# The scores of a retention's first 128 keys from float32r halves instead of float32

## The chip, the cores and the metric

The kernel runs on one core of one Trainium2 chip. The metric is the time of one execution on the device in microseconds; the number given for a kernel is the median of its runs. A profile is one execution recorded by the hardware profiler; its span runs from the first to the last instruction. Names of engines: PE is TensorE's matmul stream, PEld its weight loads, DVE is VectorE, ACT is ScalarE, POOL is GpSimd, SP is SyncE, which here only issues transfers.

## What is computed

The reference is one inference step of a two-layer streaming encoder for a prompt of 256 frames and 32 further frames of a running stream. Layer 0 mixes tokens by gated spatial mixing, layer 1 by retention with 8 heads; behind each comes a SwiGLU network, and every residual sum is normalised. All data are float32. The retention, cut to what matters here:

```python
q = rope(heads(q, RET_DK), pos) * (RET_DK ** -0.5)       # RET_DK = 256
k = rope(heads(k, RET_DK), pos)
v = heads(v, RET_DV)                                     # RET_DV = 512
...
scores = jnp.einsum('bhqd,bhkd->bhqk', q, k) * decay[None]
intra = jnp.einsum('bhqk,bhkv->bhqv', scores, v)
cross = jnp.einsum('bhqd,bhdv->bhqv', q, s0) * inner[None, :, :, None]
s_new = blk_decay[None, :, None, None] * s0 + jnp.einsum('bhkd,bhkv->bhdv', k * zeta[None, :, :, None], v)
```

The kernel takes the prompt's 256 frames as one block with masked decay, so the scores of a head are: the first 128 keys with all 256 queries, the second 128 keys with the last 128 queries, and 32 sample keys with 32 sample queries.

## The kernel before

**Float32 through halves.** A float32 product of two operands runs on TensorE at a fraction of the speed of its reduced form float32r. Nearly all products of the kernel are therefore made of three float32r products: an operand is split into a high half (a cast to float32r, on ACT, L437) and a low half (the float32 value less the high half, on DVE, L438), and high x high, low x high and high x low are summed in PSUM (`step`, L106 to L108). The function `split` makes both halves. A few small products are left in plain float32; each shows in the profile as two records.

**The stream of weights.** All weights lie in one packed array in the order in which they are used, 8 blocks of 128 x 128 to a chunk. `prep` fetches a chunk on SP's queue into `raw`, and `split` makes `whi` and `wlo`; it is called three chunks ahead. A chunk feeds 24 matmuls. ACT's cast of a chunk waits until TensorE has let go of an older chunk's tile. Every chunk costs ACT one cast and DVE one subtraction of 1024 columns.

**The order.** TensorE's instructions are in the order in which the program writes them. On ACT and DVE a scheduler orders them when the program is built; each engine works through its list in order. A matmul names the results that it waits for, and what stands behind it on TensorE waits with it.

**The retention.** Its projection `b_in` makes, for each head, two row blocks of k, two of q (128 rows by 288 columns each: 256 prompt and 32 sample frames), four of v and four of the gate. When a block of 16 products of three is done, `evac` is called and then a tick is counted; `core.after(n, f)` calls f after n ticks, so a tick is the time of one block. When both blocks of k or of q are there, `turn` rotates them on DVE (`rope`, L655 to L660: rt1 and rt2, the first 128 rows of the result, rt1 and rt2 again, the second rows) into a float32 tile `rk` or `rq`. For k it transposes the rows (`tk`), which POOL's queue writes to DRAM (`k_room`) and reads back turned (`kw`); from these `k_split` makes `kh`, `kl` and `ks`, with casts on ACT (L741, L747) and subtractions on DVE (L743, L749). For q it makes `qf` and its two halves `qi`, and asks for `scores` two ticks later (three in head 0, whose `turn` is itself two ticks late).

**The scores.** `scores` (L757 to L761) makes the three score blocks with six float32 products, two for each block, one for each 128 rows of q and k. DVE multiplies them with the decay (`pf`, L766 to L768), ACT and DVE split the result, and `attend` and `attend_prompt` multiply it with v, with products of 512 columns (L623 is the helper `wide`, which views the columns in fours).

**The small tiles.** `PostNorm.tmp` gives a tile of 128 x 320 float32 from a ring of six (tag `tmp` in the pool `lnp`). The normalisations use it for sums and squares; the start of `b_in` uses it for the corrected blocks `fix`. From the turn of head 0 to the normalisation's end behind `b_out` nothing else used it.

## Time and profile before

| what | value |
|---|---|
| median of 3 runs | 2780.95 us (2780.55 to 2782.05) |
| span of the profiled execution | 2779.0 us |
| instructions | 51384 |
| PE, DVE, ACT, POOL busy | 100%, 61%, 45%, 5% |
| HBM, over the span | 184 GB/s |
| matmul of 288 columns, recorded length | 288 to 289 ns |
| scores of all heads, first and last start | 1211.5 to 1810.2 us |

The profiled execution has no other time than its span; the median of the runs is 1.95 us above it, for what lies before the first and behind the last instruction. Matmul records overlap: the next one starts before the recorded length is over. What a matmul takes from TensorE is therefore read from start to start. In a row of the timeline stand the start, the length, the engine, the line, the operation with what it writes and reads, and how many were merged; idle time of the engine before it stands in brackets with what ended it.

### The profile page before, as it was taken

What the parts mean: (1) busy time and instruction counts of PE and PEld (TensorE: products, weight loads), DVE (VectorE), ACT (ScalarE), POOL (GpSimd) and SP (SyncE); (2) the same over time, 40 slices, a digit from 0 to 9 for tenths busy, and PEclk for the clock granted to TensorE, in tenths of its full rate; (3) what the DMA queues carried; (4) which work ended last, traced back from release to release, by engine and by line L of the source; (5) the groups of instructions that cost most, each with busy time, mean ns of one, the idle gap of its engine ahead of it and who ended that gap; (6) DMA issues with size and microseconds to landing.
All of it is one profiled execution on the core that took longest, in us unless ns stands there. A gap on an engine that the chain in (4) does not pass through costs nothing.

```text
span 2779.0 us, 51384 instructions
## 1 busy us (share of the span) xinstructions
PE 2767.0 (100%) x21574; PEld 2754.2 (99%) x21574; DVE 1691.7 (61%) x2414; ACT 1236.9 (45%) x1635; POOL 141.4 (5%) x241
## 2 busy tenths in 40 slices
PE   9999999999999999999999999999999999999998
PEld 9999999999999999999999999999999999999998
DVE  6688964445444466867765666767854445444465
ACT  5455553333343344644543444445643433333343
POOL 1100000000000000022200111200000000000001
PEclk9999999999999999999999999999999999999999
DMA  8655555555555555577765666765555555555553
GB/s 285 213 186 166 169 172 174 172 173 175 175 174 173 175 177 176 168 224 232 234 194 175 195 220 215 229 194 172 169 173 175 175 174 172 172 174 174 175 175 125
DMA packets 146584, 515.49 MB, mean 185 GB/s; under 512 B 18016, under 2 KB 20336, under 8 KB 146320
## 3 DMA queue, kind: packets, MB, share of 16 engines
q1 hardware_dynamic: 131984, 473.47, 52.3%
q0 software_dynamic: 14224, 38.59, 4.5%
q8 instruction: 168, 2.75, 0.4%
q14 instruction: 64, 0.52, 0.1%
q10 hardware_dynamic: 144, 0.15, 0.0%
HBM read 486.98 MB, written 25.17 MB: 184 GB/s over the span
## 4 chain that ended last, share of the span: by engine, by line
PE 99%; DVE 0%; issue 0%; ACT 0%; DVEq 0%; POOL 0%; POOLq 0%
PE af_in L107 13%; PE af_in L108 13%; PE af_in L106 13%; PE ab_in L107 7%; PE ab_in L106 7%; PE ab_in L108 7%; PE af_out L108 6%; PE af_out L106 6%; PE af_out L107 6%; PE aa_in L108 2%; PE ab_out L108 2%; PE ab_out L106 2%; PE aa_in L107 2%; PE aa_in L106 2%; PE ab_out L107 2%; PE aa_out L107 1%
## 5 line engine op out<-in xcount | busy, mean ns | idle before, releaser
L438 DVE TENSOR_TENSOR wlo<-raw,whi 128x1024 fp32r<-128x1024 f32 (+1 forms) x892 | 1086.1, 1219 | 871.5 <-ACT whi L437 866.5
L437 ACT CAST whi<-raw 128x1024 fp32r<-128x1024 f32 (+1 forms) x892 | 931.6, 1046 | 1376.6 <-PE af_in L107 326.6
L107 PE MATMUL af_in<-xl,whi 128*128 128x288 f32 (+1 forms) x2816 | 813.9, 289 | 0.0
L108 PE MATMUL af_in<-xh,wlo 128*128 128x288 f32 (+1 forms) x2816 | 813.7, 289 | 0.0
L106 PE MATMUL af_in<-xh,whi 128*128 128x288 f32 (+1 forms) x2816 | 813.0, 289 | 0.0
L108 PEld LDWEIGHTS af_in<-xh,wlo 128*128 128x128 f32 x2816 | 527.7, 187 | 0.0
L107 PEld LDWEIGHTS af_in<-xl,whi 128*128 128x128 f32 x2816 | 527.7, 187 | 0.0
L106 PEld LDWEIGHTS af_in<-xh,whi 128*128 128x128 f32 x2816 | 527.7, 187 | 0.0
L107 PE MATMUL ab_in<-xl,whi 128*128 128x288 f32 (+1 forms) x1536 | 444.3, 289 | 0.0
L106 PE MATMUL ab_in<-xh,whi 128*128 128x288 f32 (+1 forms) x1536 | 444.2, 289 | 0.0
L108 PE MATMUL ab_in<-xh,wlo 128*128 128x288 f32 (+1 forms) x1536 | 443.6, 289 | 0.0
L106 PE MATMUL af_out<-hh,whi 128*128 128x288 f32 x1408 | 405.9, 288 | 0.0
L107 PE MATMUL af_out<-hl,whi 128*128 128x288 f32 x1408 | 405.9, 288 | 0.0
L108 PE MATMUL af_out<-hh,wlo 128*128 128x288 f32 x1408 | 405.9, 288 | 0.0
L107 PEld LDWEIGHTS ab_in<-xl,whi 128*128 128x128 f32 x1536 | 287.9, 187 | 1.1
L106 PEld LDWEIGHTS ab_in<-xh,whi 128*128 128x128 f32 x1536 | 287.9, 187 | 0.9
L108 PEld LDWEIGHTS ab_in<-xh,wlo 128*128 128x128 f32 x1536 | 287.8, 187 | 0.0
L106 PEld LDWEIGHTS af_out<-hh,whi 128*128 128x128 f32 x1408 | 263.8, 187 | 0.0
L107 PEld LDWEIGHTS af_out<-hl,whi 128*128 128x128 f32 x1408 | 263.8, 187 | 0.0
L108 PEld LDWEIGHTS af_out<-hh,wlo 128*128 128x128 f32 x1408 | 263.8, 187 | 0.0
L106 PE MATMUL aa_in<-xh,whi 128*128 128x288 f32 x512 | 148.3, 290 | 0.0
L108 PE MATMUL aa_in<-xh,wlo 128*128 128x288 f32 x512 | 147.7, 288 | 0.0
(242 smaller groups left out, 2896.1 us busy)
## 6 DMA issues: line engine op xcount, KB each, us to landing
raw<-in_wpack_dram SPq DMA_DIRECT2D x887, 512.0 KB, 3.4
v_room<-tv POOLq DMA_DIRECT2D x32, 144.0 KB, 4.9
of<-o_room POOLq DMA_DIRECT2D x32, 144.0 KB, 4.8
vw<-v_room POOLq DMA_DIRECT2D x8, 512.0 KB, 5.9
out_st_s_dram<-sso POOLq DMA_DIRECT2D x16, 256.0 KB, 2.8
o_room<-to POOLq DMA_DIRECT2D x8, 512.0 KB, 3.6
out_st_p_dram<-so POOLq DMA_DIRECT2D x16, 256.0 KB, 5.2
y<-in_xT_dram SPq DMA_DIRECT2D x8, 288.0 KB, 5.1
```

The costliest lines, as they stand in the source:

```text
L106: mm(ps, hi, xh, start=first, stop=False)
L107: mm(ps, hi, xl, start=False, stop=False)
L108: mm(ps, lo, xh, start=False, stop=last)
L437: nc.scalar.copy(hi, f)
L438: nc.vector.tensor_tensor(lo, f, hi.bitcast(F32), ALU.subtract)
```

## The change

Every head's k and q, as far as the first score block needs them, are split into halves right behind the rotation: k's first 128 columns of both row blocks in one split, q's 256 prompt columns in a split for each row block. The six halves (two of k, four of q) lie in the ring of small tiles of the normalisations. The first score block is then made of six float32r products in the view in fours: for each of the two row blocks high x high, q's low with k's high, and q's high with k's low. The other two score blocks stay in float32.

```diff
+    def room(self, name, dt=F32R):
+        return self.lnp.tile([P, ROW], dt, tag="tmp", name=name, bufs=6)
+
     def tmp(self, name, dt=F32):
-        return self.lnp.tile([P, ROW], dt, tag="tmp", name=f"{name}_{self.gi}", bufs=6)[:, LEAD:LEAD + NT]
+        return self.room(f"{name}_{self.gi}", dt)[:, LEAD:LEAD + NT]
...
                 if isk:
                     self.kr = r
+                    self.kt = [ln.room(f"kt{i}_{h}")[:, 40:40 + 2 * P].rearrange("p (d n) -> p d n", d=2) for i in range(2)]
+                    split(nc, *self.kt, r[:, :, :P])
...
                     self.qr = r
+                    self.qt = [[ln.room(f"qt{i}{d}_{h}")[:, LEAD:LEAD + NP] for i in range(2)] for d in range(2)]
+                    for d in range(2):
+                        split(nc, *self.qt[d], r[:, d, :NP])
...
                 for d in range(2):
-                    mm(b[:, 0:NP], self.kr[:, d, 0:P], self.qr[:, d, 0:NP], start=d == 0, stop=d == 1)
+                    for i, (j, q) in enumerate(((0, 0), (0, 1), (1, 0))):
+                        wide(b[:, 0:NP], self.kt[j][:, d, :], self.qt[d][q], start=d == 0 and i == 0, stop=d == 1 and i == 2)
```

In the built program the instructions of TensorE, POOL and SP keep their order but for the two float32 products that become six; ACT's list has three casts more a head and DVE's three subtractions more, and in head 2 one pair of neighbours on DVE is exchanged.

## The prediction, made before the result was known

> **What bounds the kernel now.** The page of the kernel before was read first, then who waits for whom on TensorE, then the stretches around the scores of each head, engine by engine.

> ```profile
> span 2779.0 us, 51384 instructions
> PE 2767.0 (100%) x21574; PEld 2754.2 (99%) x21574; DVE 1691.7 (61%) x2414; ACT 1236.9 (45%) x1635; POOL 141.4 (5%) x241
> ...
> PEclk9999999999999999999999999999999999999999
> ...
> PE 99%; DVE 0%; issue 0%; ACT 0%; DVEq 0%; POOL 0%; POOLq 0%
> ```

> TensorE is busy all the time at full clock, and the chain that ended last is TensorE for 99%. Its waits are one, at the start:

> ```profile
> PE warm L937 <- POOL g_nrm L486: 1.0, 1, 1.0
> ```

> So TensorE is the clock of this kernel: what it is spared is gained whole, and whatever it must wait is lost whole, since nothing later has slack to give it back. VectorE at 61% looks free, but this is a mean. Seven microseconds around the start of the scores look like this (the heads with numbers 1, 2 and 7; columns: PE, PEld, DVE, ACT, POOL busy, clock, DMA share, GB/s):

> ```profile
> 1270.00:1277.00 7.00, 7.00 (x56) 6.90 (x55) 6.60 (x15) 4.05 (x7) 0.00 (x0) 1.00 0.67 218
> 1327.00:1334.00 7.00, 7.00 (x56) 6.90 (x55) 6.60 (x17) 3.96 (x7) 0.00 (x0) 1.00 0.62 205
> ...
> 1805.00:1812.00 7.00, 7.00 (x56) 6.89 (x55) 6.35 (x17) 4.58 (x9) 0.00 (x0) 1.00 0.47 162
> ```

> There VectorE is over 90% busy, right where the change gives it work on which TensorE will wait.

> **The products, removed and added.** Scores of head 2 on TensorE (start, length, operation; the x4 are two fp32 products of two records each):

> ```profile
> 1330.73 0.29 PE L108 MATMUL ab_in<-xh,wlo 128*128 128x288 f32 x1
> 1330.86 1.02 PE L757 MATMUL sc<-rq,rk 128*128 128x256 f32 x4
> 1331.72 0.61 PE L759 MATMUL sc<-rq,rk 128*128 128x128 f32 x4
> ```

> What is removed holds TensorE from 1330.86 to 1331.72: 0.86 us a head. In its place stand six float32r products of 256 columns. The trace has that form once, in the sample's mixing, two products from 139.58 to 139.82, so 0.12 us each; beside it float32r of 288 columns and of 512:

> ```profile
> 139.58 0.41 PE L546 MATMUL smix<-g_v,g_w 96*128 96x256 f32 x2
> 139.82 0.30 PE L106 MATMUL aa_in<-xh,whi 128*128 128x288 f32 x1
> 139.96 0.29 PE L107 MATMUL aa_in<-xl,whi 128*128 128x288 f32 x1
> 140.09 0.29 PE L108 MATMUL aa_in<-xh,wlo 128*128 128x288 f32 x1
> ...
> 1395.97 0.39 PE L623 MATMUL os<-whi,qi 128*64 128x512 f32 x1
> 1396.19 0.39 PE L623 MATMUL os<-wlo,qi 128*64 128x512 f32 x1
> ```

> Start to start, 288 columns take 0.13 us and 512 take 0.22, half of which is 0.11. I take 0.12, bounds 0.11 and 0.13: six take 0.72 us (0.66 to 0.78). Alone that is a gain of 0.14 us a head, 1.1 us over eight. L759 and L761 stay as they are, with their one change back to float32r.

> **The splits, and who waits.** Each head adds three casts on ScalarE and three subtractions on VectorE, 256 columns each.

> ```profile
> L437 ACT CAST xh<-y 128x288 fp32r<-128x288 f32 x64 | 26.6, 430 | 17.0 <-PE af_in L108 8.1 <-DMA y<-in_xT_dram 5.4 <-PE ab_in L108 3.4
> L766 DVE TENSOR_TENSOR pf<-sc,dec 128x256 f32<-128x256 f32 x8 | 3.3, 417 | 0.0
> ```

> That is 0.42 us for a subtraction (L766 has its size) and about 0.40 for a cast (430 ns for 288 columns): 10 us in all on each engine, free as long as nobody waits. k's halves are made before q is there at all, and q's first halves with rq; nobody waits for these. q's second low half is the case. As built, VectorE's order in heads 1 to 7 is: rt2q, low half of q's first 128 rows, rq, qf, wlo, four kl, two ks, low half of q's second rows, qi. TensorE needs that last half for its fifth product. VectorE and ScalarE before, head 2:

> ```profile
> 1327.49 0.45 DVE L659 TENSOR_TENSOR rt2q<-ab_in,r_cs 128x288 f32<-128x288 f32 x1
> 1327.97 0.46 DVE L660 TENSOR_TENSOR rq<-rt1q,rt2q 128x288 f32<-128x288 f32 x1
> 1328.46 0.22 DVE L712 TENSOR_TENSOR qf<-rq,r_inn 128x64 f32<-128x64 f32 x1
> 1328.97 1.23 DVE L438 TENSOR_TENSOR wlo<-raw,whi 128x1024 fp32r<-128x1024 f32 x1 [0.28 <-ACT whi L437]
> 1330.11 1.14 DVE L743 SCALAR_TENSOR_TENSOR kl<-kw,r_zt,kh 128x128 fp32r<-128x128 f32 x4
> 1331.26 0.61 DVE L749 SCALAR_TENSOR_TENSOR ks<-kw,r_zt,ks 32x128 fp32r<-32x128 f32 x2
> 1331.90 0.23 DVE L438 TENSOR_TENSOR qi<-qf,qi 128x64 fp32r<-128x64 f32 x1
> ```

> ```profile
> 1327.88 1.05 ACT L437 CAST whi<-raw 128x1024 fp32r<-128x1024 f32 x1 [1.94 <-PE ab_in L107]
> 1328.84 0.24 ACT L437 CAST qi<-qf 128x64 fp32r<-128x64 f32 x1
> 1328.98 0.91 ACT L741 ACTIVATE kh<-kw,r_zt 128x256 fp32r<-128x256 f32 x2
> 1329.79 1.03 ACT L747 ACTIVATE ks<-kw,r_zt 32x256 fp32r<-32x256 f32 x2
> ```

> Step by step. The first low half goes between rt2q and rq and moves rq and qf by some 0.25 us; VectorE sat idle 0.28 us before wlo, which waits for whi, so wlo still starts at 1328.97 (without that idle, everything behind is 0.25 later). ScalarE's cast of q's second rows goes ahead of its qi and moves kh and ks by 0.31: the first kh then ends about 1329.8, before kl needs it at 1330.11, and ks ends about 1331.13, before VectorE's ks at 1331.26. So the ks still end at 1331.87 and the new half takes qi's place at 1331.90 and ends at 1332.32. (Lower bound: four kl in 1.14 us and two ks in 0.61 make 0.27 for each further one, so a half that follows at that spacing starts at 1331.79, 0.11 earlier.) The scores start at 1330.86: the fifth product, due four products later at 1331.34, stands and waits. Behind it on TensorE's queue stand the sixth, the other scores, and the whole of the projection's stream.

> [...]

> How soon TensorE goes on after a VectorE result, the trace shows at the end of the kernel:

> ```profile
> 2762.25 0.46 DVE L236 TENSOR_TENSOR y<-af_out,y 128x288 f32<-128x288 f32 x1 [5.47 <-PE af_out L108]
> ...
> 2762.76 0.75 PE L305 MATMUL m<-y,one 128*128 128x288 f32 x2
> 2762.76 0.30 PEld L305 LDWEIGHTS m<-y,one 128*128 128x128 f32 x2 [0.27 <-DVE y L236]
> ```

> Result at 2762.71, product at 2762.76: 0.05 us, and its weight load starts only then, so the first product after a wait may cost up to one more product (0 to 0.13); I take 0.05. [...]

> So in head 2 the fifth product starts at 1332.37, the wait is 1.03 us, two products and the restart end at 1332.66, where L759 started at 1331.72 before: 0.94 us lost. Where qi stands in the other heads, first and last of the seven:

> ```profile
> 1274.20 0.59 PE L757 MATMUL sc<-rq,rk 128*128 128x256 f32 x2
> 1275.30 0.23 DVE L438 TENSOR_TENSOR qi<-qf,qi 128x64 fp32r<-128x64 f32 x1
> ...
> 1808.71 0.81 PE L757 MATMUL sc<-rq,rk 128*128 128x256 f32 x3
> 1809.77 0.23 DVE L438 TENSOR_TENSOR qi<-qf,qi 128x64 fp32r<-128x64 f32 x1
> ```

> 1.10 and 1.06 us behind the scores' start against 1.04 in head 2. Head 1 has more: k's low half is put ahead of the second transpose of k there, so POOL's k_room and kw transfers go out some 0.3 us later, and ScalarE's kh already waits for them:

> ```profile
> 1272.97 0.91 ACT L741 ACTIVATE kh<-kw,r_zt 128x256 fp32r<-128x256 f32 x2 [0.55 <-DMA kw<-k_room]
> ```

> That moves kl, ks and the half by 0.3: 1.3 us for head 1. In heads 4, 5 and 6 the same move falls behind ScalarE's own 0.31 and costs nothing. Head 0 waits a tick longer and has its halves early:

> ```profile
> 1197.52 0.22 DVE L438 TENSOR_TENSOR qi<-qf,qi 128x64 fp32r<-128x64 f32 x1
> ...
> 1211.46 1.02 PE L757 MATMUL sc<-rq,rk 128*128 128x256 f32 x4
> ```

> Nearly 14 us: it gains its 0.14. The tiles cost nothing: six halves fill the ring of six, and the next head's splits wait only for products of a head whose scores began 50 us before and more (1274.20 and 1330.86 above are neighbours). SP's queue is not touched; wlo behind the half comes 0.4 us later for blocks needed several us on.

> **The sum.** 6 x 0.94 + 1.3 - 0.14 = 6.8 us: a span of 2785.8 for 2779.0. The median of the runs is 2780.95, 1.95 above the span for what lies around it, so 2787.8 us, 0.24% slower. Low end of every term (half 0.11 earlier, restart 0, products 0.11, head 1 like the rest): 0.76 a head, 5.1 in all, 2786.1. High end (restart 0.13, products 0.13, the first half not hidden by 0.1): 1.15 a head, 1.5 for head 1, 8.3 in all, 2789.3.

> **Rivals.** *Not slower: TensorE isn't held at the fifth product.* It decides from the moment at which the half ends before 1331.3, a microsecond earlier than worked out, as when VectorE reaches it ahead of kl and ks. Then only the products count: 2780.95 - 1.1 = 2779.8, no measurable change. For it speaks that q itself is ready at 1328.43, 2.4 us ahead; against it, that VectorE works in order and wlo, kl and ks fill the time until 1331.87. A hold of about half the size would end at 2783.5, also within 0.2%.

> *Slower still: ScalarE's chain decides.* If its casts take 0.13 us more than worked out, VectorE's ks waits for ScalarE's ks past 1331.26; a further 0.36 (one more cast ahead of it) costs 7 x 0.36 = 2.5 us, 2790.3. The float32r products at the pace of the fp32 records (0.215) would give nearly the same: two behind the wait at 0.19 more in seven heads, 0.57 in head 0, 1.9 us, 2789.7; the row of 256 columns at 0.12 speaks against it.

> **How the numbers follow.** Forecast 0.74, with a range of its own from 2786.0 to 2789.5; no hold or half a hold 0.18; slower still 0.08. 0.2%, about what a measurement of this kernel can tell from no change, is 5.6 us, so slower begins at 2786.5, close under the forecast: of its 0.74 I count 0.67 as slower and 0.07 as within. Slower 0.67 + 0.08 = 0.75; within 0.07 and 0.16 of the first rival's 0.18, 0.23; faster 0.02, what is left for a gain that no row shows. The range is from 2785.0 to 2790.5.

> **What would show it.** A wait of TensorE for VectorE's split of qt in seven heads, about 1 us each and more in head 1, none in head 0; six products at 0.12 where they do not wait; VectorE's half starting as the second ks ends, 1.05 us behind the scores' start. Wrong it would be if TensorE shows no idle time there, or waits at another product or for ScalarE, or if waits appear at wlo.

## The result, and the profile after

| what | before | after |
|---|---|---|
| median of 5 runs each, taken in turn | 2782.05 us (2780.55 to 2782.60) | 2792.01 us (2790.93 to 2798.14) |
| ratio, 95% interval | | 1.004 [1.003, 1.005] |
| span of the profiled execution | 2779.0 us | 2789.9 us |

The kernel became 0.4% slower, 10.0 us, where 6.8 had been worked out. The sign was forecast; the time lies 1.5 us above the range. The page of the kernel after (span, busy times, and the shares of the chain that ended last), and its whole answer on what TensorE waits for (us in total, times, longest):

```profile
span 2789.9 us, 51460 instructions
...
PE 2769.3 (99%) x21590; PEld 2755.5 (99%) x21590; DVE 1699.2 (61%) x2438; ACT 1245.1 (45%) x1659; POOL 141.4 (5%) x241
...
PE 95%; DMA 2%; DVE 2%; issue 1%; POOL 0%; ACT 0%; SPq 0%; DVEq 0%; POOLq 0%; ACTq 0%
```

```profile
PE sc L626 <- DVE qt L441: 8.1, 7, 1.8
PE warm L946 <- POOL g_nrm L489: 1.0, 1, 1.0
PE aa_in L108 <- DVE wlo L441: 0.3, 1, 0.3
```

TensorE waits seven times for VectorE's `qt`, once in each of heads 1 to 7, 8.1 us in all; and the chain, 99% TensorE before, now goes through VectorE and, for 2%, through transfers. The 0.3 us at `aa_in` lie at the start of the kernel, before anything that the change touches. The timeline of the kernel after shows two heads, 3 and 5 (an x4 on TensorE is the first four products, the x2 behind it the fifth and the sixth):

```profile
1389.80 1.13 DVE L751 SCALAR_TENSOR_TENSOR kl<-kw,r_zt,kh 128x128 fp32r<-128x128 f32 x4
...
1390.50 0.62 PE L626 MATMUL sc<-qt,kt 128*128 128x256 f32 x4
...
1390.95 0.60 DVE L757 SCALAR_TENSOR_TENSOR ks<-kw,r_zt,ks 32x128 fp32r<-32x128 f32 x2
1391.56 0.43 DVE L441 TENSOR_TENSOR qt<-rq,qt 128x256 fp32r<-128x256 f32 x1
...
1392.05 0.50 PE L626 MATMUL sc<-qt,kt 128*128 128x256 f32 x2 [0.92 <-DVE qt L441]
...
1392.38 0.27 PE L768 MATMUL sc<-rq,rk 128*128 128x128 f32 x1
...
1676.04 0.91 ACT L749 ACTIVATE kh<-kw,r_zt 128x256 fp32r<-128x256 f32 x2 [1.04 <-DMA kw<-k_room]
...
1676.42 0.62 PE L626 MATMUL sc<-qt,kt 128*128 128x256 f32 x4
1676.59 1.14 DVE L751 SCALAR_TENSOR_TENSOR kl<-kw,r_zt,kh 128x128 fp32r<-128x128 f32 x4 [0.77 <-ACT kh L749]
...
1677.74 0.60 DVE L757 SCALAR_TENSOR_TENSOR ks<-kw,r_zt,ks 32x128 fp32r<-32x128 f32 x2
...
1678.36 0.43 DVE L441 TENSOR_TENSOR qt<-rq,qt 128x256 fp32r<-128x256 f32 x1
...
1678.84 0.50 PE L626 MATMUL sc<-qt,kt 128*128 128x256 f32 x2 [1.79 <-DVE qt L441]
...
1679.17 0.39 PE L768 MATMUL sc<-rq,rk 128*128 128x128 f32 x2
```

Head 3 is the forecast: four `kl`, two `ks`, then the half, 1.06 us behind the scores' start, and the fifth product waits for it. From the first product to the next score block (L768) pass 1.88 us, where 0.86 had passed before: 1.02 lost, 0.94 forecast. Head 5 is not: ScalarE's `kh` stood 1.04 us for the transfer `kw`, VectorE's `kl` 0.77 for `kh`, so that the half came 1.94 us behind the start and the block took 2.75. By the starts of all heads, the block took 0.69 us in head 0, 1.88 in heads 1, 3 and 6, and 2.29, 2.18, 2.75 and 1.95 in heads 2, 4, 5 and 7. Less 0.86 each, that is 8.6 us.

The rest of the 10.9 us between the spans shows in stretches of 3.41 us around heads 3 and 5 (columns: the stretch, its length, busy time of PE, PEld, DVE, ACT, POOL, then the granted clock, the DMA share and GB/s):

```profile
1389.99:1393.40 3.41, 2.49 (x22) 2.29 (x21) 3.33 (x10) 2.17 (x4) 0.00 (x0) 1.00 0.49 163
...
1673.29:1676.70 3.41, 3.41 (x30) 3.41 (x29) 2.48 (x6) 2.16 (x5) 0.00 (x0) 1.00 0.64 211
1676.70:1680.12 3.42, 1.63 (x14) 1.43 (x14) 3.33 (x9) 2.51 (x5) 0.00 (x0) 1.00 0.47 157
1680.12:1683.53 3.41, 3.41 (x16) 3.41 (x16) 1.46 (x6) 0.63 (x2) 0.58 (x1) 0.50 0.56 189
1683.53:1686.94 3.41, 3.41 (x29) 3.41 (x29) 1.09 (x1) 1.06 (x1) 0.00 (x0) 1.00 0.02 8
```

Behind head 5's long wait TensorE was granted half its clock for 3.41 us: 16 matmuls where a full stretch has 29 or 30, half of 3.41, 1.7 us lost. Behind head 3's wait it was not. So 8.6 + 1.7 = 10.3 us. The other 0.6 are not from the heads: head 0's scores start 0.8 us later than before, from differences in the first 134 us, which the change does not touch, and 0.2 us are gained elsewhere.

### The profile page after: what moved, and what is told of

Same layout as the page of the kernel before. It is cut to its first block, busy times and chain, and to the rows that moved or that the text cites. A ratio compares the mean times of both kernels' runs of the same rounds, so it can differ in the third digit from the quotient of the medians.

```text
span 2789.9 us, 51460 instructions
## 1 busy us (share of the span) xinstructions
PE 2769.3 (99%) x21590; PEld 2755.5 (99%) x21590; DVE 1699.2 (61%) x2438; ACT 1245.1 (45%) x1659; POOL 141.4 (5%) x241
## 3 DMA queue, kind: packets, MB, share of 16 engines
q8 instruction: 168, 2.75, 0.4%
## 4 chain that ended last, share of the span: by engine, by line
PE 95%; DMA 2%; DVE 2%; issue 1%; POOL 0%; ACT 0%; SPq 0%; DVEq 0%; POOLq 0%; ACTq 0%
PE af_in L107 13%; PE af_in L106 13%; PE af_in L108 13%; PE af_out L108 6%; PE af_out L107 6%; PE af_out L106 6%; PE ab_in L107 6%; PE ab_in L106 6%; PE ab_in L108 6%; PE ab_out L107 2%; PE ab_out L106 2%; PE ab_out L108 2%; PE aa_in L108 2%; PE aa_in L106 2%; PE aa_in L107 2%; PE aa_out L107 1%
## 5 line engine op out<-in xcount | busy, mean ns | idle before, releaser
L107 PE MATMUL af_in<-xl,whi 128*128 128x288 f32 (+1 forms) x2816 | 814.7, 289 | 0.0
L106 PE MATMUL af_in<-xh,whi 128*128 128x288 f32 (+1 forms) x2816 | 814.5, 289 | 0.0
L108 PE MATMUL af_in<-xh,wlo 128*128 128x288 f32 (+1 forms) x2816 | 813.8, 289 | 0.0
L107 PEld LDWEIGHTS af_in<-xl,whi 128*128 128x128 f32 x2816 | 528.4, 188 | 0.0
L106 PEld LDWEIGHTS af_in<-xh,whi 128*128 128x128 f32 x2816 | 528.4, 188 | 0.0
L108 PEld LDWEIGHTS af_in<-xh,wlo 128*128 128x128 f32 x2816 | 528.3, 188 | 0.0
L107 PE MATMUL ab_in<-xl,whi 128*128 128x288 f32 (+1 forms) x1536 | 445.5, 290 | 0.0
L106 PE MATMUL ab_in<-xh,whi 128*128 128x288 f32 (+1 forms) x1536 | 445.4, 290 | 0.0
L108 PE MATMUL ab_in<-xh,wlo 128*128 128x288 f32 (+1 forms) x1536 | 444.9, 290 | 0.0
L106 PE MATMUL af_out<-hh,whi 128*128 128x288 f32 x1408 | 406.3, 289 | 0.0
L107 PE MATMUL af_out<-hl,whi 128*128 128x288 f32 x1408 | 406.3, 289 | 0.0
L108 PE MATMUL af_out<-hh,wlo 128*128 128x288 f32 x1408 | 406.3, 289 | 0.0
L107 PEld LDWEIGHTS ab_in<-xl,whi 128*128 128x128 f32 x1536 | 288.9, 188 | 1.0
L106 PEld LDWEIGHTS ab_in<-xh,whi 128*128 128x128 f32 x1536 | 288.9, 188 | 0.8
L108 PEld LDWEIGHTS ab_in<-xh,wlo 128*128 128x128 f32 x1536 | 288.8, 188 | 0.0
L108 PEld LDWEIGHTS af_out<-hh,wlo 128*128 128x128 f32 x1408 | 264.2, 188 | 0.0
L106 PEld LDWEIGHTS af_out<-hh,whi 128*128 128x128 f32 x1408 | 264.1, 188 | 0.0
L107 PEld LDWEIGHTS af_out<-hl,whi 128*128 128x128 f32 x1408 | 264.1, 188 | 0.0
L108 PE MATMUL aa_in<-xh,wlo 128*128 128x288 f32 x512 | 148.1, 289 | 0.5 <-DVE wlo L441 0.3
L106 PE MATMUL aa_in<-xh,whi 128*128 128x288 f32 x512 | 148.5, 290 | 0.0
```

The lines of the kernel that those rows point to most:

```text
L106: mm(ps, hi, xh, start=first, stop=False)
L107: mm(ps, hi, xl, start=False, stop=False)
L108: mm(ps, lo, xh, start=False, stop=last)
```

## The experiments

Theory 1: TensorE waits because q's last low half stands behind `kl` and `ks` on VectorE. Theory 2: what a wait has beyond head 3's comes from transfers, either (2a, the Theory 2 of the second text) because k's split delays them or (2b, the rival there) because they land at differing times. Theory 3: an idle time of about half a 3.41 us stretch halves TensorE's clock (in the profile after, 1.79 us idle in head 5 came ahead of a stretch at 0.50, 0.92 us in head 3 did not). The rivals are that the splits' load, the tiles or the products cost the time. The first four experiments ran beside one set of 25 runs of the kernel before, the next four beside 15, the last beside 15.

**Order on VectorE.** The split of k's turned columns is asked for one tick later.

```diff
-                core.after(self.wait, self.k_split)
+                core.after(self.wait + 1, self.k_split)
```

> Edit: the split of k's turned columns (kh, kl, ks) is asked for one tick later, so that VectorE makes q's last low half and qi ahead of the four kl and two ks; nothing else moves. Theory 1 (order: TensorE stands at the fifth product only because q's last low half is queued behind kl and ks on VectorE): the half is ready 0.3 to 0.7 us before the scores start, no wait of sc for qt is left, six products take 0.69 us where the two float32 ones took 0.86, so 8 x 0.17 = 1.4 us below the kernel before: about 2780.7 us, no half-clock stretch. Rival 1 (load: the three casts and three subtractions a head, or their tiles, cost the time wherever they stand): stays at 2790 to 2792. Rival 2 (the wait moves: kl and ks, now 0.65 us later, are late for their own products, the update of the state): sc loses its wait, another group of TensorE takes one on, and the time lies between.

Measured: 2780.4 us against 2781.69, ratio 0.9995 [0.9986, 1.0005]. TensorE has no wait in the heads. The timeline around head 3:

```profile
1385.92 0.42 DVE L441 TENSOR_TENSOR qt<-rq,qt 128x256 fp32r<-128x256 f32 x1
...
1386.40 1.13 DVE L751 SCALAR_TENSOR_TENSOR kl<-kw,r_zt,kh 128x128 fp32r<-128x128 f32 x4
...
1386.62 0.85 PE L626 MATMUL sc<-qt,kt 128*128 128x256 f32 x6
...
1387.31 0.61 PE L768 MATMUL sc<-rq,rk 128*128 128x128 f32 x4
```

The half is ready 0.28 us before the scores, `kl` comes behind it, and six products take 0.69 us. In head 4 of this run `kh` waited for its transfer until 0.2 us behind the scores' start, and TensorE did not feel it. Theory 1 holds; rival 1 falls, since all splits and products are still there, and rival 2, since no other wait took the place of this one.

**k's transfers first.** k's split goes behind the second transpose and the transfers.

```diff
                 if isk:
                     self.kr = r
                     self.kt = [...]
-                    split(nc, *self.kt, r[:, :, :P])
                     nc.scalar.copy(...)
                     self.k_move()
+                    split(nc, *self.kt, r[:, :, :P])
```

> Edit: k's split into halves is put behind k's second transpose and its transfers; all else as in the changed kernel. Theory 2 (what the hold has beyond 1.2 us in heads 2, 4 and 5, by 0.4, 0.3 and 0.9 us, comes from k's transfers to DRAM and back, which leave 0.7 to 1.2 us later behind k's split, so that ScalarE's kh waits for kw): fifth product 1.2 us behind the fourth in all seven heads, sc 1.6 us shorter. Theory 3 (clock: the hold of 2.07 us in head 5 set TensorE to half clock for 3.4 us, 1.7 us lost): no half-clock stretch, 1.7 us more. Both: 3.3 us below the changed kernel, 2788.7. Rival (the transfers' landing jitters by itself, and the half-clock stretch comes at random): heads with 1.5 us and over stay, within 1 us of the changed kernel's time.

Measured: 2793.6 us, ratio 1.0041 [1.0026, 1.0056]: no better, and two half-clock stretches in the profile where none had been expected. Yet the transfers that fetch `kw` do leave two to three us earlier in heads 4, 5 and 6, and land 2.0, 2.7 and 2.9 us ahead of the scores' start, where 1.0, 0.4 and 1.4 were left in the profile after. What had held them up shows on VectorE in head 4, in the kernel before (first row; scores start at 1590.10) and in the changed one (the other two; 1594.10):

```profile
1576.74 0.47 DVE L727 STREAM_TRANSPOSE tk<-rk 128x288 f32<-128x288 f32 x1
...
1581.59 0.43 DVE L441 TENSOR_TENSOR kt<-rk,kt 128x256 fp32r<-128x256 f32 x1 [0.75 <-ACT kt L440]
1581.93 0.47 DVE L735 STREAM_TRANSPOSE tk<-rk 128x288 f32<-128x288 f32 x1
```

k's low half stood 0.75 us for ScalarE's cast, and k's second transpose, behind it, came 12.2 us ahead of the scores instead of 13.4. With this edit it comes 13.4 us ahead again. But the fifth product starts 1.77, 1.36, 1.20, 2.80, 2.13, 2.00 and 1.27 us behind the fourth in heads 1 to 7. The timeline of ScalarE ahead of head 4's scores (start 1594.25) says why:

```profile
1589.35 0.41 ACT L440 CAST qt<-rq 128x256 fp32r<-128x256 f32 x1
1592.92 1.05 ACT L440 CAST whi<-raw 128x1024 fp32r<-128x1024 f32 x1 [3.16 <-DMA raw<-in_wpack_dram]
1593.88 0.40 ACT L440 CAST qt<-rq 128x256 fp32r<-128x256 f32 x1
1594.18 0.91 ACT L749 ACTIVATE kh<-kw,r_zt 128x256 fp32r<-128x256 f32 x2
```

Here a chunk of weights landed late; its cast stood 3.16 us, and behind it q's cast, `kh`, `kl` and the half. In heads 5 and 6 a chunk's cast stood 2.27 and 2.36 us for its transfer, in heads 1 and 2 `kh` stood 0.88 and 0.33 us for `kw`. So Theory 2a holds in part, k's split does delay `kw` in heads 4 to 6; but it is not the whole cause of the long waits, and which transfer is late differs. Whether the earlier `kw` made the chunks late is not tested, and the edit also moved q's `qi` behind `kh` on ScalarE in four heads.

**Splits alone.** All halves are made, the block is made in float32, and no product reads them.

```diff
-                    for i, (j, q) in enumerate(((0, 0), (0, 1), (1, 0))):
-                        wide(b[:, 0:NP], self.kt[j][:, d, :], self.qt[d][q], ...)
+                    mm(b[:, 0:NP], self.kr[:, d, 0:P], self.qr[:, d, 0:NP], start=d == 0, stop=d == 1)
```

> Edit: all splits of k and q are made as in the changed kernel, but the first score block is made of the two float32 products again, so that nothing reads the halves. Theory 1 (only the wait of TensorE for the last half costs): TensorE has no wait in the heads, the time of the kernel before, 2782 +-1. Rival 1 (the splits' load on VectorE and ScalarE, or their tiles, delay something else): 2 us and more above the kernel before, with waits of TensorE at wlo, kl, qi or sd.

Measured: 2781.57 us, ratio 0.9998 [0.9989, 1.0008]. The one wait of TensorE in the heads, and ScalarE's timeline ahead of it:

```profile
PE sc L765 <- DVE rq L663: 0.3, 1, 0.3
```

```profile
1587.97 1.05 ACT L440 CAST whi<-raw 128x1024 fp32r<-128x1024 f32 x1 [5.01 <-PE ab_in L107]
1588.93 0.40 ACT L440 CAST qt<-rq 128x256 fp32r<-128x256 f32 x1
```

The casts, subtractions and tiles cost nothing that shows, as Theory 1 had it. The 0.3 us are in head 4, where ScalarE's cast of a chunk stood 5.0 us and behind it the casts of q's rows; VectorE, in the meantime, waited with the rotation (L663) that the float32 products read.

**Low halves last.** TensorE makes the two float32 blocks first, then the four products without q's low halves, then the two with them.

```diff
-                for d in range(2):
-                    for i, (j, q) in enumerate(((0, 0), (0, 1), (1, 0))):
-                        wide(...)
...
+                prods = [(d, j, q) for j, q in ((0, 0), (1, 0), (0, 1)) for d in range(2)]
+                for i, (d, j, q) in enumerate(prods):
+                    wide(b[:, 0:NP], self.kt[j][:, d, :], self.qt[d][q], start=i == 0, stop=i == 5)
```

> Edit: the order of TensorE alone: the two float32 score blocks first (0.61 us), then the four products that need no low half of q, then the two that do. Theory 1 (the half is ready at a moment that VectorE alone sets, 1.07 us behind the scores' start where kw is in time, and TensorE waits only for what is missing by then): the products with q's low halves are due 1.07 us behind the start, so no wait or 0.1 us in heads 1, 3, 6, 7, and 0.4, 0.3, 0.9 in heads 2, 4, 5; sc falls by 7 x 1.07 = 7.5 us, no half-clock stretch (1.7 us): about 2783. Rival 3 (the float32r products, or the change between float32 and float32r, cost the time by themselves): stays above 2788.

Measured: 2786.07 us, ratio 1.0018 [1.0009, 1.0027], 3 us above what was expected. Head 3 on TensorE:

```profile
1388.73 0.61 PE L765 MATMUL sc<-rq,rk 128*128 128x128 f32 x4
...
1389.46 1.21 PE L626 MATMUL sc<-qt,kt 128*128 128x256 f32 x6
1390.50 0.30 PE L106 MATMUL ab_in<-xh,whi 128*128 128x288 f32 x1
```

Where transfers were in time (heads 1, 3, 4) the half again starts 1.07 us behind the scores' start, and of the 1.02 us lost in such a head 0.18 are left (1.77 us from the scores' start to the next product of the projection, 1.59 in the kernel before). The miss is head 6: `kw` landed 1.0 us behind the scores' start, the last of the six products, which reads the late half, started 2.6 us behind the one before it, and a half-clock stretch followed. Rival 3 falls.

**The changed kernel again.**

> The changed kernel itself, without an edit. Theory 2b (what the hold has beyond 1.2 us is the landing of transfers, which differs from run to run: ScalarE's casts stand behind a wait for a late weight chunk or a late kw, and q's half behind those): about 1.2 us between the fourth and the fifth product again in heads 1, 3 and 6, but other heads than 2, 4 and 5 over 1.4 us. Theory 2a (the changed order of k's transposes does it): the same heads 2, 4 and 5. Theory 3 (TensorE's clock is halved for 3.41 us where over half of one stretch of a 3.41 us grid is idle; idle times of 1.96, 2.02, 2.48 and 2.68 us inside one stretch did it so far, 1.66 did not): a half-clock stretch only behind a hold of 1.8 us and more. Time 2790 to 2793 without such a stretch, 1.7 us more for each.

Measured: 2794.51 us (2792.61 to 2797.60, 5 runs) against 2781.68, ratio 1.0047 [1.0034, 1.0059]. The fifth product starts 1.20 us behind the fourth in heads 2, 3 and 5, 1.27 in 7, 1.38 in 1, 1.47 in 6, and 3.00 in head 4. ScalarE ahead of head 4's scores (start 1592.89), and the stretches around them:

```profile
1593.45 0.91 ACT L749 ACTIVATE kh<-kw,r_zt 128x256 fp32r<-128x256 f32 x2 [1.94 <-DMA kw<-k_room]
```

```profile
1592.09:1595.50 3.41, 1.43 (x12) 1.23 (x10) 1.73 (x7) 2.00 (x5) 0.00 (x0) 1.00 0.77 258
1595.50:1598.91 3.41, 2.66 (x13) 2.67 (x14) 2.48 (x6) 1.17 (x2) 0.00 (x0) 0.50 0.14 24
1598.91:1602.32 3.41, 3.41 (x16) 3.41 (x16) 1.01 (x4) 0.63 (x2) 0.59 (x1) 0.50 0.59 184
1602.32:1605.74 3.42, 3.42 (x29) 3.42 (x28) 1.22 (x1) 1.05 (x1) 0.00 (x0) 1.00 0.00 0
```

Heads 2 and 5, late in the first profile, are on time here, and heads 1 and 6 are late by 0.2 and 0.3 us, so the lateness does come and go, as Theory 2b has it, though heads 1 and 6 had been expected on time. Head 4 is late in both, as Theory 2a has it. The half clock came behind the one hold over 1.8 us, for two stretches, the first of which still held idle time.

**Scores later.** One tick more of distance.

```diff
-                    core.after(self.wait, self.scores)
+                    core.after(self.wait + 1, self.scores)
```

> Edit: the scores are asked for three ticks behind q's turn instead of two (four in head 0), so that TensorE reaches them some 6 us later; VectorE's and ScalarE's orders move with it. Theory 1 (order and distance: the half is ready 1.5 us behind the scores' old start): no wait of sc for qt, six products in 0.69 us, 1.4 us below the kernel before: about 2780.3 us; late transfers, up to 2.7 us so far, are covered too. Rival 1 (load): 2788 and more. Rival 2 (the later scores make the multiplication with v, or the transfers of the result, late): sc without a wait, but a wait of TensorE at sd, qi or in b_out, over 2782.

Measured: 2780.74 us against 2781.68, ratio 0.9995 [0.9986, 1.0004]: no wait of TensorE in the heads, six products in 0.69 us in all of them. ScalarE's own waits for `kw` in this run:

```profile
ACT kh L749 <- DMA kw<-k_room: 9.5, 5, 4.6
```

The longest wait, 4.6 us, is in head 7; no other profile here shows more than 1.9. It is not a slow landing: in this order VectorE makes k's second transpose of head 7 at 1799.15 us, 6.5 us later than in the first experiment, and `kw` then takes 5.2 us from issue to landing. With a tick of distance nobody on TensorE noticed.

**Longer holds.** Some or all `kl` are made twice, with the same values.

```diff
                     for d in range(2):
-                        nc.vector.scalar_tensor_tensor(self.kl[:, j, d], ...)
+                        for _ in range(1 + j):
+                            nc.vector.scalar_tensor_tensor(self.kl[:, j, d], ...)
```

> Edit: the two subtractions kl of the second 128 rows are made twice (the same values), 0.53 us more on VectorE ahead of q's last half. Theory 1: the fifth product starts 1.75 us behind the fourth in heads that had 1.2, 7 x 0.53 = 3.7 us more than the changed kernel. Theory 3: idle times of about 1.65 us in a stretch of the clock's grid set no half clock, so only heads with late transfers get it, at most one more than in the changed kernel: 2795.5 to 2799. Rival (any hold over 1.5 us halves the clock, or at random): three and more half-clock stretches, over 2800.

Measured: 2799.91 us, ratio 1.0065 [1.0051, 1.0079], above the 2795.5 to 2799 expected. The time from the fourth to the fifth product was 1.73 to 1.80 us in heads 2, 3, 4 and 7, as expected, but 2.48, 2.83 and 2.31 in heads 1, 5 and 6, and behind these three the clock was halved. Head 6 and head 7:

```profile
1766.07:1769.49 3.42, 1.73 (x15) 1.73 (x16) 3.39 (x10) 1.25 (x2) 0.00 (x0) 1.00 0.42 138
1769.49:1772.90 3.41, 3.41 (x16) 3.41 (x15) 1.22 (x5) 0.63 (x2) 0.57 (x1) 0.50 0.59 196
1824.10:1827.51 3.41, 2.00 (x17) 1.80 (x15) 3.38 (x11) 3.10 (x7) 0.00 (x0) 1.00 0.65 223
1827.51:1830.93 3.42, 3.31 (x27) 3.31 (x28) 2.79 (x8) 0.63 (x2) 0.00 (x0) 1.00 0.31 96
```

At most two drops had been expected, and three is what the rival had. But all three stand behind late halves, and none behind the four holds of 1.73 to 1.80 us, as it would if any hold over 1.5 us halved the clock. The second kernel repeats all four (`range(2)` in both rows):

> Edit: all four subtractions kl are made twice (the same values), 1.06 us more on VectorE ahead of q's last half. Theory 1: the fifth product starts 2.3 us behind the fourth, 7 x 1.06 = 7.4 us more than the changed kernel: 2799.4. Theory 3: 2.1 us of idle time halve the clock where one stretch of the 3.41 us grid holds over half of it, that is for some six positions in ten, about four of seven heads, 1.7 us each: 2804 to 2807 in all. Rival (the half clock needs longer idle times, and came by chance in head 5): 2799 to 2801.

Measured: 2806.46 us, ratio 1.0091 [1.0076, 1.0107], in the range of Theory 3. Four of seven heads (3, 4, 5, 7) were followed by half-clock stretches, one of them by two. Heads 3 and 6 had the same hold, 2.25 us from the fourth product to the fifth:

```profile
1392.97:1396.39 3.42, 1.45 (x13) 1.45 (x14) 3.34 (x10) 1.07 (x2) 0.00 (x0) 1.00 0.40 147
1396.39:1399.80 3.41, 3.41 (x16) 3.41 (x16) 1.28 (x5) 0.63 (x2) 0.58 (x1) 0.50 0.64 196
...
1771.85:1775.27 3.42, 1.94 (x17) 1.94 (x18) 3.39 (x10) 0.35 (x1) 0.00 (x0) 1.00 0.28 114
1775.27:1778.68 3.41, 3.41 (x29) 3.41 (x28) 1.01 (x4) 1.65 (x3) 0.57 (x1) 1.00 0.63 197
```

Head 3's lay almost wholly in one stretch of the grid, head 6's was cut by a boundary at 1771.85; only the first halved the clock. Between these two the length did not decide, the place did: TensorE was busy for 1.45 us of head 3's stretch and for 1.94 us of head 6's.

**The better order again.** The kernel of the first experiment, with more runs.

> The kernel with the split of k's turned columns one tick later, once more and with more runs. Theory 1 (six products in 0.69 us for 0.86, no wait): 8 x 0.17 = 1.4 us, 0.05% under the kernel before, with no wait of sc for qt and no half-clock stretch in the heads. Rival (its 1.3 us of the first look were the scatter of the runs): the same as the kernel before or above it.

Measured: 2780.71 us against 2781.20, ratio 0.9999 [0.9990, 1.0008], no wait of the scores for `qt`. The margin is thin: in head 6 of this profile the half ended 0.32 us behind the scores' start, 0.14 us before the fifth product; and one of the 11 runs took 2786.25 us, for which there is no trace. The kernel is 0.4% below the changed kernel, and with 1.3 us and 0.5 us below the kernel before in its two series not to be told from it by time. What the change can give, 8 x 0.17 = 1.4 us, is seen only in the trace.

## Why the prediction was wrong

What held. TensorE is the clock of the kernel (99% busy), and what it waits is lost whole: of the 10.9 us between the spans 8.6 lie in the score blocks, where it waits 8.1 us for `qt`. The six products, unhindered, take 0.69 us for 0.86, a gain of 0.17 us a head (0.14 forecast). The splits cost nothing by themselves. One half is late, the one named, because VectorE's order puts it behind `kl` and `ks`; in the heads on time it starts 1.06 us behind the scores' start (1.04 forecast), at the end of the second `ks`. In head 3 the `ks` end at 1391.55 (1390.95 and 0.60) and the half starts at 1391.56, in head 5 at 1678.34 (1677.74 and 0.60) and 1678.36; the forecast's lower bound, a start 0.11 us earlier, did not come in these. Of the rivals, "not slower" came out as worked out once its condition was made true: with the half ahead of `kl` and `ks` the wait is gone, and a gain of 1.1 us had been forecast for that.

A small miss. The restart was taken at 0.05 us and costs 0.10: the fifth and sixth product take 0.33 us from 1392.05 to 1392.38, two of the six unhindered ones 0.23. With it, and the half 0.02 us later than forecast, a head on time loses 1.02, not 0.94: 7 x 1.02 - 0.17 = 7.0 us, against the forecast's 6.8.

The step that failed is the one that set the half's time in every head from one execution of the kernel before, with a delay by k's transfers of "some 0.3 us" in head 1 alone, while "in heads 4, 5 and 6 the same move falls behind ScalarE's own 0.31 and costs nothing". In the profile after, head 1 was on time, and heads 2, 4, 5 and 7 lost 0.41, 0.30, 0.87 and 0.07 us more than head 3, 1.6 in all, in the first three with ScalarE's `kh` waiting for `kw`. Two things lie behind it.

The first is the term for the changed order, which was sized too small. Of k's halves the prediction said "nobody waits for these". But VectorE itself waited for ScalarE's cast before it could make k's low half:

```profile
DVE kt L441 <- ACT kt L440: 1.7, 3, 0.8
```

These are heads 4, 5 and 6. Counted from the scores' start, k's second transpose came 1.2, 0.7 and 1.1 us later there than in the kernel before, and the transfers of `kw` left 1.3, 0.8 and 1.3 us later, not 0.3. The second is that `kw` lands at differing times: in heads 1 to 7 of the eleven profiles it took 3.1 to 6.1 us from issue to landing, and in head 2, where it left 0.6 us later than in the kernel before, 5.2 us against 4.5. Before the change no wait of TensorE hung on these transfers near the scores; the change put a result behind them on which TensorE stands. The rival "ScalarE's chain decides" had the right place for this and the wrong cause (longer casts). The order's part is shown by the second experiment, where the transposes are back in their place and `kw` is in time in heads 4 to 6; that the rest comes and goes is shown by the second profile of the changed kernel. How the 1.6 us divide between the two is not settled, nor why weight chunks were late in the second experiment.

And a term was missing. Head 5's hold, 2.07 us from the fourth to the fifth product, cost more than its length: 1.7 us in the first profile for the half-clock stretch behind it. The prediction worked out no price for the clock at all. Together 7.0 + 1.6 + 1.7 = 10.3 of the 10.9 us between the spans, and both of the last two terms differ between the two profiles of the changed kernel. That fits its scatter, 7 us over its five runs where the kernel before had 2 beside it (5 over the 25 runs beside the first experiments): the run of 2798.14 us has a granted clock of 0.997, that of 2790.97 one of 0.999. It is not shown run by run, since only one run of each set was traced.

## What to carry to other kernels

Where one engine sets the time, a new operand of it is not priced by its own length but by everything that stands ahead of it in the queue of the engine that makes it, transfers included, and by what it pushes back there itself, as k's low half did with k's transposes; leave a distance that covers their scatter (3.1 to 6.1 us from issue to landing here), not their time in one profile. Before moving a consumer, look for the producer's place: here one tick less haste for work that nobody was waiting for removed the whole loss, with 0.14 us to spare in the tightest head traced. And price a stall twice, once for its length and once for what the clock does behind it: here 1.7 us for a full stretch at 0.50.

## What the runs showed of the hardware

```profile
1273.32:1276.74 3.42, 1.93 (x17) 1.73 (x15) 2.92 (x10) 2.79 (x6) 0.00 (x0) 1.00 0.56 211
1276.74:1280.15 3.41, 3.41 (x28) 3.41 (x29) 2.89 (x8) 0.85 (x3) 0.58 (x1) 1.00 0.27 70
```
